# One kernel, two transformer blocks: loads of gates and activations in the expert down stage moved from SyncE's queue to ScalarE's

## The chip, the cores and the metric

The kernel runs on one core of one Trainium2 chip. The metric is the device time of one execution in microseconds (us); less is better. The time before is the median of three runs, 2463.1 us.

## What is computed

The reference is two transformer blocks on a sequence of 512 tokens with model width 1024, all in float32. The first block mixes tokens with attention and a gated linear scan and ends in a large sparse expert layer (`peer_ffn`); the second block has a pooling and gating mixer, a convolutional feed-forward layer and a gate. The change lies in the expert layer alone:

```
q = (xi @ w_q).reshape(n, 8, 2, 128)
s = einsum('nhpc,hpkc->nhpk', q, sub_keys)
...
idx  = ...                                   # 16 of 128*128 experts for each of 8 heads
gate = softmax(best_s)
act  = gelu(einsum('nd,nhkd->nhk', xi, u[idx]))
out  = einsum('nhk,nhkd->nd', gate * act, v[idx])
```

Each token uses 8 x 16 = 128 of the 16384 experts. `u` and `v` are tables of 16384 rows of 1024 numbers.

## The kernel before, in words

**Two ways through the expert layer.** The first 384 tokens (three tiles of 128) go a dense way: the activation of every expert is computed, and a matrix of gates, mostly zeros, is multiplied in. The experts are taken in 128 columns j of 128 experts. The last 128 tokens go a sparse way: `rows()` gathers for every token the rows of `u` and `v` it needs (`gather`, line 802, an indirect DMA issued by GpSimd) and VectorE multiplies and adds them (lines 815 and 823). These gathers run beside the dense work.

**Split operands.** A float32 matrix product is made of three products of float32r parts: high by high, high by low, low by high. Each weight tile of 512 KB is loaded raw by SyncE (`load_raw`, line 58, tile `wraw`), and `split` makes, in two halves each, the high part by a ScalarE cast (line 73, `whi`) and the low part by a VectorE subtraction (line 74, `wlo`). The raw tiles have 3 + 5 = 8 buffers in the expert layer, `whi` and `wlo` four half-tile buffers each, so two weight tiles are ready or in use at a time. `split` keeps its last cast in `c.step`, and `paced` makes an instruction wait for that cast.

**The up stage** (`route_and_up`) computes for j = 0 to 95 the activations gelu(x u_j) and stores them to a DRAM buffer `Ad`, four columns to a store (line 1022, from tile `ast`). The matrix of gates is built meanwhile and stored to a DRAM buffer `Gd`, 16 tokens to a store.

**The down stage** (`down`) walks through 160 steps in the order of `down_order`: eight "up" steps for a fresh block of columns, then 24 "down" steps for three kept blocks, then eight for the fresh one, four times over. An up step is 24 matmuls of 128 x 384 (line 97) and a Gelu on ScalarE (line 790, tile `fresh`). A down step is 18 matmuls of 128 x 512 (line 1105), which add w_j v_j into six PSUM banks, w_j being activations times gates. Each group of four down steps needs one `weigh`, emitted two steps ahead (`WEIGH = 2`): VectorE multiplies activations by gates (line 1070, tile `wt`), ScalarE casts the product (line 186, `wh`), VectorE makes its low part (line 187, `wl`). Before that, `load` brings the activations of the group back from `Ad` (line 1064, tile `at`, 768 KB, two buffers) and, once in two groups, the gates of a block of eight columns from `Gd` (line 1061, tile `gt`, 1536 KB in runs of 512 bytes, two buffers). `load` is emitted eight steps ahead (`LOAD = 8`), both loads go through SyncE's queue, and both are paced. Fresh blocks need no `at`: their activations are still in SBUF.

```
while to_load and to_load[0][0] - s <= LOAD:
    load(to_load.pop(0)[1])
while to_weigh and to_weigh[0][0] - s <= WEIGH:
    weigh(to_weigh.pop(0)[1])
```

**Order.** Each engine, and each engine's queue of DMA issues, works strictly in its own order. The order within an engine is fixed by the framework's scheduler when the kernel is built: it goes by the order of the code, but puts an instruction that it reckons ready before an earlier one that it does not. So SyncE issues the raw weight loads as soon as one of the eight buffers is reckoned free, ahead of their use, and the loads of `at` and `gt` stand between them in one queue.

Of the kernel before, what the change touches and what calls it, by code (L numbers as in the profile page):

```python
# [8 lines left out]
F32 = mybir.dt.float32  # L9
# [11 lines left out]
P = 128  # L21
# [163 lines left out]
def split_plain(c, hi, lo, x):  # L185
    c.nc.scalar.copy(hi, x)
    c.nc.vector.tensor_tensor(lo, x, hi.bitcast(F32), ALU.subtract)
# [545 lines left out]
DT = ND * P  # L733
GT = 16
NG = DT // GT
JG = 4
JG2 = 2 * JG
NS = 96
KEEP = 1
LOAD = 8  # L740
WEIGH = 2
ROWS = 4
AFTER = 4
# [13 lines left out]
def peer_block(c):  # L757
# [4 lines left out]
    with ExitStack() as ctx:  # L762
# [78 lines left out]
        with ExitStack() as vctx:  # L841
            down(c, vctx, aux, up, bank)
# [198 lines left out]
def down(c, ctx, aux, up, bank):  # L1041
    nc, tc, I, X = c.nc, c.tc, c.I, c.X
    wk = ctx.enter_context(tc.tile_pool(name="pv", bufs=2))
    acc = [aux(f"acc{i}") for i in range(2 * ND)]
    acts, gts, ws = {}, {}, {}
    rate = (2 * P - c.n_rows) / (NKEYS + (NKEYS - NS) - 8)
    due = 0.0

    def turn():
        nonlocal due  # L1050
        due += rate
        while due >= 1:
            next(c.rows, None)
            due -= 1

    def load(j):

        j0, b0 = j // JG2 * JG2, j % JG2
        if b0 == 0:
            gts[j0] = wk.tile([P, NG, JG2, GT], F32, name="gt")  # L1060
            c.paced(nc.sync.dma_start(out=gts[j0], in_=c.Gd[:, :, j0:j0 + JG2, :].rearrange("n i j g -> i n j g")))
        if j0 not in acts:
            ws[j] = wk.tile([P, JG, DT], F32, name="at")
            c.paced(nc.sync.dma_start(out=ws[j], in_=c.Ad[j // JG]))  # L1064

    def weigh(j):
        j0, b0 = j // JG2 * JG2, j % JG2
        at = acts[j0][:, b0:b0 + JG, :] if j0 in acts else ws[j]
        wt = wk.tile([P, JG, NG, GT], F32, name="wt", bufs=1)
        nc.vector.tensor_tensor(wt, at.rearrange("p j (n g) -> p j n g", g=GT),  # L1070
                                gts[j0][:, :, b0:b0 + JG, :].rearrange("p n j g -> p j n g"), ALU.mult)
        w = wt.rearrange("p j n g -> p j (n g)")
        ws[j] = [wk.tile([P, JG, DT], F32R, name=n) for n in ("wh", "wl")]
        split_plain(c, *ws[j], w)

    steps = [(what, j) for what, j0 in c.order for j in range(j0, j0 + JG2)]
    groups = [(s, j) for s, (what, j) in enumerate(steps) if what == "down" and j % JG == 0]
    to_load, to_weigh = list(groups), list(groups)
    n_done, batch = 0, []
    for s, (what, j) in enumerate(steps):  # L1080
        while to_load and to_load[0][0] - s <= LOAD:
            load(to_load.pop(0)[1])
        while to_weigh and to_weigh[0][0] - s <= WEIGH:
            weigh(to_weigh.pop(0)[1])
        if what == "up":
            if j % JG2 == 0:
                acts[j] = c.keep.tile([P, JG2, DT], F32, name="fresh")
            up(j, acts[j // JG2 * JG2][:, j % JG2, :])
            turn()
            continue  # L1090
        wh, wl = ws[j // JG * JG]
        vh, vl = next(c.peer_w)
        batch.append((j % JG, vh, vl))
        n_done += 1
        turn()
        if n_done == NKEYS - 1:
            continue

        last2 = n_done == NKEYS
        for hf in range(2):  # L1100
            for t in range(ND):
                tk = slice(t * P, (t + 1) * P)
                for bi, (jb, bh, bl) in enumerate(batch):
                    for pi, (x, y) in enumerate(((wh, bh), (wh, bl), (wl, bh))):
                        nc.tensor.matmul(acc[2 * t + hf], x[:, jb, tk], y.row(hf), start=n_done == 1 and pi == 0,  # L1105
                                         stop=last2 and bi == len(batch) - 1 and pi == 2)
        batch = []
    for _ in c.rows:
        pass
    for q in range(2):  # L1110
        for t in (ND, *range(ND)):
            if t < ND:
                y = wk.tile([P, 512], F32, tag=("at", "gt")[(q * ND + t) % 2], name="y")
                nc.scalar.copy(y, acc[2 * t + q])
            else:
                y = c.acc3[:, q * 512:(q + 1) * 512]
            o = bank("yt")
            for k in range(4):
                nc.tensor.transpose(o[:, k * P:(k + 1) * P], y[:, k * P:(k + 1) * P], c.ident)
            xs = X[:, 4 * q:4 * q + 4, t * P:(t + 1) * P]  # L1120
            nc.vector.tensor_tensor(xs, xs, o.rearrange("p (k n) -> p k n", k=4), ALU.add)
# [383 lines left out]
```

## Time and profile before

| | |
|---|---|
| runs | 2460.37, 2463.1, 2471.28 us; median 2463.1 |
| the profiled execution's own time | 2468.12 us |
| its span, from first to last instruction | 2466.4 us |
| TensorE busy (matmul) | 2402.0 us, 97% of the span |
| VectorE busy | 1758.2 us, 71% |
| ScalarE busy | 1194.7 us, 48% |
| GpSimd busy | 367.3 us, 15% |
| mean granted TensorE clock | 0.987 of full speed |

The profile counts an engine as busy while its instructions run; waiting, branching and issuing DMAs do not count. PE is TensorE's matmuls, PEld its weight loads, DVE VectorE, ACT ScalarE, POOL GpSimd, SP SyncE; a "q" behind an engine's name is its sequencer, which waits and issues DMAs. "a <- b" in a list of waits says that a stood idle until b was done. The down stage lies at about 962 to 1640 us of the span.

### The profile page before, as it was taken

The numbers are of one execution on the slowest core, as the hardware profiler recorded it, in microseconds if no ns is written. First come the engines' busy times: TensorE is split into PE (matmuls) and PEld (weight loads), VectorE is DVE, ScalarE is ACT, GpSimd is POOL, SyncE is SP. The second block draws the span as 40 slices with busy tenths as digits, with TensorE's granted clock in tenths as the row PEclk, the third lists the DMA queues.
The fourth block names the chain that finished last, engine by engine and source line by source line (L and its number), as shares of the span: only waits on it lengthen the run. The fifth ranks groups of instructions, "written<-read, shape, count | busy, mean of one in ns | idle before, by whom it ended". The sixth has DMA issues, their size and how long they took to land.

```text
span 2466.4 us, 34671 instructions
## 1 busy us (share of the span) xinstructions
PE 2402.0 (97%) x12603; PEld 2084.6 (85%) x12603; DVE 1758.2 (71%) x3426; ACT 1194.7 (48%) x2155; POOL 367.3 (15%) x260
## 2 busy tenths in 40 slices
PE   8999899999999999999999998999999999999998
PEld 7887578999999999888778788878888888888888
DVE  5775659999899886886676775866764456777436
ACT  5434553446788995433333333335433335544335
POOL 0000000001333323333242342420000000000000
PEclk9999999999999999999999999999999999999999
DMA  4210033356999999988888889953232232233332
GB/s 138 69 52 26 27 128 137 104 187 202 335 358 348 329 332 361 364 299 295 309 283 289 321 291 311 311 175 106 87 98 94 95 102 96 94 97 98 94 105 103
DMA packets 170297, 471.81 MB, mean 191 GB/s; under 512 B 14060, under 2 KB 66157, under 8 KB 166798
## 3 DMA queue, kind: packets, MB, share of 16 engines
q1 hardware_dynamic: 133262, 335.37, 39.8%
q0 software_dynamic: 36864, 134.23, 15.7%
q8 instruction: 99, 1.62, 0.3%
q14 instruction: 72, 0.59, 0.1%
HBM read 421.31 MB, written 48.23 MB: 190 GB/s over the span
## 4 chain that ended last, share of the span: by engine, by line
PE 62%; DMA 9%; issue 6%; DVE 5%; POOL 2%; ACT 1%; SPq 0%; DVEq 0%; POOLq 0%; ACTq 0%
PE mm L97 49%; PE acc L1105 8%; DMA at<-Ad 3%; DMA row<-in_v_t_dram,ev 3%; PE G L987 3%; POOL row L802 2%; DVE wlo L74 1%; DMA row<-in_peer_u_dram,eu 1%; DMA wraw<-in_v_t_dram 1%; DVE acc L823 1%; PE sc L886 1%; DMA gt<-Gd 1%; DVE row L815 0%; SPq L1064 0%; DVE eq L939 0%
## 5 line engine op out<-in xcount | busy, mean ns | idle before, releaser
L73 ACT CAST whi<-wraw 128x512 fp32r<-128x512 f32 (+3 forms) x902 | 547.4, 609 | 900.8 <-PE mm L97 521.3
L74 DVE TENSOR_TENSOR wlo<-wraw,whi 128x512 fp32r<-128x512 f32 (+3 forms) x902 | 595.4, 670 | 260.6 <-ACT whi L73 256.6
L97 PE MATMUL mm<-hi,whi 128*128 128x384 f32 (+3 forms) x2016 | 721.4, 363 | 16.3 <-ACT fresh L790 9.3
L97 PE MATMUL mm<-lo,whi 128*128 128x384 f32 (+3 forms) x2016 | 717.9, 361 | 0.7 <-DVE lo L182 0.5
L97 PE MATMUL mm<-hi,wlo 128*128 128x384 f32 (+3 forms) x2016 | 717.0, 361 | 0.4 <-DVE wlo L74 0.4
L97 PEld LDWEIGHTS mm<-hi,whi 128*128 128x128 f32 (+1 forms) x2016 | 376.3, 188 | 56.2 <-ACT fresh L790 10.2
L97 PEld LDWEIGHTS mm<-hi,wlo 128*128 128x128 f32 (+1 forms) x2016 | 376.0, 188 | 38.2 <-DVE wlo L74 1.7
L97 PEld LDWEIGHTS mm<-lo,whi 128*128 128x128 f32 (+1 forms) x2016 | 376.1, 188 | 38.1 <-issue 1.7
L1105 PE MATMUL acc<-wlo,wh 128*128 128x512 f32 x768 | 304.0, 396 | 20.9 <-DVE wlo L74 20.7
L802 POOL DMA_INDIRECT row<-in_peer_u_dram,eu x128 | 168.4, 1316 | 930.0 <-DMA wraw<-in_u_t_dram 544.4
L1105 PE MATMUL acc<-whi,wl 128*128 128x512 f32 x768 | 302.2, 394 | 0.0
L802 POOL DMA_INDIRECT row<-in_v_t_dram,ev x128 | 198.7, 1552 | 333.6 <-ACT whi L73 239.2
L1105 PE MATMUL acc<-whi,wh 128*128 128x512 f32 x768 | 248.1, 394 | 0.0
L823 DVE SCALAR_TENSOR_TENSOR acc<-row,act,acc 128x1024 f32<-128x1024 f32 x128 | 163.8, 1280 | 46.0 <-DMA row<-in_v_t_dram,ev 46.0
L1105 PEld LDWEIGHTS acc<-wlo,wh 128*128 128x128 f32 x768 | 146.3, 191 | 56.1 <-DVE wlo L74 25.7
L815 DVE SCALAR_TENSOR_TENSOR row<-row,hn 128x1024 f32<-128x1024 f32 x128 | 155.6, 1218 | 26.6 <-DMA row<-in_peer_u_dram,eu 26.3
L1105 PEld LDWEIGHTS acc<-whi,wh 128*128 128x128 f32 x768 | 146.0, 190 | 30.7
L1105 PEld LDWEIGHTS acc<-whi,wl 128*128 128x128 f32 x768 | 146.3, 190 | 30.3
L984 ACT ACTIVATE oa<-oa,tr 128x128 f32<-128x128 f32 x384 | 122.6, 393 | 21.5 <-DVE oa L982 21.1
L987 PE MATMUL G<-ob,oa 128*128 128x128 f32 x768 | 113.1, 277 | 1.2 <-ACT oa L984 1.2
L987 PEld LDWEIGHTS G<-ob,oa 128*128 128x128 f32 x768 | 108.9, 191 | 2.3 <-ACT oa L984 2.2
L988 ACT COPY gst<-G 128x512 f32<-128x512 f32 x96 | 102.1, 1070 | 16.1 <-PE G L987 15.2
(359 smaller groups left out, 3048.6 us busy)
## 6 DMA issues: line engine op xcount, KB each, us to landing
wraw<-in_u_t_dram SPq DMA_DIRECT2D x128, 512.0 KB, 5.3
wraw<-in_v_t_dram SPq DMA_DIRECT2D x128, 512.0 KB, 7.1
Gd<-gst SPq DMA_DIRECT2D x24, 1024.0 KB, 6.3
gt<-Gd SPq DMA_DIRECT2D x16, 1536.0 KB, 13.0
wraw<-in_w_up_dram SPq DMA_DIRECT2D x44, 512.0 KB, 3.4
Ad<-ast SPq DMA_DIRECT2D x24, 768.0 KB, 5.6
at<-Ad SPq DMA_DIRECT2D x24, 768.0 KB, 12.3
wraw<-in_w_pq_dram SPq DMA_DIRECT2D x16, 512.0 KB, 4.2
```

The lines of the kernel that those rows point to most:

```text
L73: self.step = nc.scalar.copy(hi[i], x)
L74: nc.vector.tensor_tensor(lo[i], x, hi[i].bitcast(F32), ALU.subtract)
L97: nc.tensor.matmul(o, a, b, start=first and ps == 0 and i == 0, stop=last and ps == 2 and i == n - 1)
L802: i = nc.gpsimd.indirect_dma_start(out=t, out_offset=None, in_=table, in_offset=bass.IndirectOffsetOnAxis(ap=idx[:, s:s + 1], axis=0))
L815: nc.vector.scalar_tensor_tensor(u, u, 1.0, hn, op0=ALU.mult, op1=ALU.mult, accum_out=c.act3[:, s:s + 1])
L823: nc.vector.scalar_tensor_tensor(c.acc3, v, c.act3[:, s:s + 1], c.acc3, op0=ALU.mult, op1=ALU.add)
L886: nc.tensor.matmul(o[:, t * P:(t + 1) * P], q[:, t * P:(t + 1) * P], keys[:, f, :], start=True, stop=True)
L984: nc.scalar.mul(oa[:, i, :], oa[:, i, :], tr[:, 2, b0 + i:b0 + i + 1])
L987: nc.tensor.matmul(o[:, i * P:(i + 1) * P], oa[:, i, :], ob[:, i, :], start=True, stop=True)
L988: nc.scalar.copy(st[:, :, b0 - t0:b0 - t0 + TB].rearrange("p j n -> p n j"), o.rearrange("p (n j) -> p n j", n=TB))
L1105: nc.tensor.matmul(acc[2 * t + hf], x[:, jb, tk], y.row(hf), start=n_done == 1 and pi == 0, stop=last2 and bi == len(batch) - 1 and pi == 2)
```

## The change

The function `load` and its distance `LOAD` go. In its place are `load_gates` and `load_acts`, each of which takes the next load from a list. Both issue their DMA from ScalarE's queue and neither is paced. Two blocks of gates and two groups of activations are loaded ahead of the first step; after that, each `weigh` of a kept group is followed by the load of activations for the kept group after next (into the buffer that it has just read), and each second `weigh` of a block by the load of gates for the block after next. The name of the change also says that the weights' low parts stay in halves; the code before has them in halves, and no line of the diff touches them.

```diff
-LOAD = 8
...
-    def load(j):
-
-        j0, b0 = j // JG2 * JG2, j % JG2
-        if b0 == 0:
-            gts[j0] = wk.tile([P, NG, JG2, GT], F32, name="gt")
-            c.paced(nc.sync.dma_start(out=gts[j0], in_=c.Gd[:, :, j0:j0 + JG2, :].rearrange("n i j g -> i n j g")))
-        if j0 not in acts:
-            ws[j] = wk.tile([P, JG, DT], F32, name="at")
-            c.paced(nc.sync.dma_start(out=ws[j], in_=c.Ad[j // JG]))
+    def load_gates():
+        j0 = gts_due.pop(0)
+        gts[j0] = wk.tile([P, NG, JG2, GT], F32, name="gt")
+        nc.scalar.dma_start(out=gts[j0], in_=c.Gd[:, :, j0:j0 + JG2, :].rearrange("n i j g -> i n j g"))
+
+    def load_acts():
+        j = ats_due.pop(0)
+        ws[j] = wk.tile([P, JG, DT], F32, name="at")
+        nc.scalar.dma_start(out=ws[j], in_=c.Ad[j // JG])
 
     def weigh(j):
...
         split_plain(c, *ws[j], w)
 
+        if j < NS and ats_due:
+            load_acts()
+        if b0 and gts_due:
+            load_gates()
+
     steps = [(what, j) for what, j0 in c.order for j in range(j0, j0 + JG2)]
     groups = [(s, j) for s, (what, j) in enumerate(steps) if what == "down" and j % JG == 0]
-    to_load, to_weigh = list(groups), list(groups)
+    to_weigh = list(groups)
+    ats_due, gts_due = [j for _, j in groups if j < NS], [j for _, j in groups if j % JG2 == 0]
+    for f in (load_gates, load_acts, load_acts, load_gates):
+        f()
     n_done, batch = 0, []
     for s, (what, j) in enumerate(steps):
-        while to_load and to_load[0][0] - s <= LOAD:
-            load(to_load.pop(0)[1])
         while to_weigh and to_weigh[0][0] - s <= WEIGH:
             weigh(to_weigh.pop(0)[1])
```

## Rows read from the trace of the kernel before

**Rows 1.** The page's first part: busy time and share of the span by engine.
```profile
PE 2402.0 (97%) x12603; PEld 2084.6 (85%) x12603; DVE 1758.2 (71%) x3426; ACT 1194.7 (48%) x2155; POOL 367.3 (15%) x260
```

**Rows 2.** Stretch, length, busy us (count) of PE PEld DVE ACT POOL, clock, DMA share, GB/s.
```profile
962.00:1640.00 678.00, 647.87 (x2971) 554.38 (x2970) 491.74 (x564) 247.37 (x374) 239.17 (x156) 0.98 0.89 307
996.00:1119.00 123.00, 123.00 (x544) 101.86 (x543) 96.48 (x121) 46.41 (x68) 42.34 (x32) 1.00 0.93 324
```

**Rows 3.** Who waited for whom in the down stage: us, times, longest us.
```profile
ACT whi L73 <- PE acc L1105: 296.1, 197, 8.4
DVE wt L1070 <- DMA at<-Ad: 68.0, 13, 10.0
...
DVE acc L823 <- DMA row<-in_v_t_dram,ev: 46.0, 33, 6.5
...
ACT wh L186 <- DVE wt L1070: 28.3, 8, 7.5
...
PE acc L1105 <- DVE wlo L74: 20.7, 9, 5.2
...
DVE wt L1070 <- DMA gt<-Gd: 11.4, 3, 4.0
...
PE mm L97 <- ACT fresh L790: 9.3, 3, 4.1
```

**Rows 4.** Six short stretches without matmuls; columns as in rows 2.
```profile
1138.80:1142.90 4.10, 0.00 (x0) 0.00 (x0) 4.10 (x4) 2.42 (x4) 0.16 (x1) 1.00 0.63 251
1178.30:1183.50 5.20, 0.02 (x1) 0.00 (x0) 2.36 (x3) 0.23 (x1) 0.00 (x0) 0.78 0.69 275
1323.90:1325.90 2.00, 0.02 (x1) 0.00 (x0) 2.00 (x3) 2.00 (x4) 0.15 (x1) 1.00 0.90 356
1359.60:1364.60 5.00, 0.00 (x0) 0.00 (x1) 2.41 (x3) 0.39 (x1) 0.00 (x0) 0.76 1.00 400
1498.90:1502.00 3.10, 0.03 (x1) 0.00 (x0) 3.10 (x4) 2.36 (x4) 0.10 (x1) 1.00 0.65 260
1537.20:1541.00 3.80, 0.02 (x1) 0.00 (x0) 2.33 (x3) 0.45 (x1) 0.00 (x0) 0.82 0.92 367
```

**Rows 5.** First and last of five slow-clock stretches behind them, and one at full clock.
```profile
1143.60:1147.00 3.40, 3.40 (x13) 3.40 (x12) 3.40 (x6) 1.30 (x3) 2.56 (x2) 0.52 0.43 64
...
1541.20:1546.40 5.20, 5.20 (x13) 4.04 (x14) 5.20 (x7) 0.62 (x1) 3.05 (x1) 0.50 0.58 202
1547.00:1552.20 5.20, 5.20 (x25) 4.27 (x24) 4.35 (x6) 2.93 (x4) 1.81 (x1) 1.00 0.61 235
```

**Rows 6.** SyncE's queue in order of time: start us, us, what it issued.
```profile
963.34 0.33 SPq L1022 DMA_DIRECT2D Ad<-ast  x1
...
968.87 0.38 SPq L1061 DMA_DIRECT2D gt<-Gd  x1
969.30 7.18 SPq L1064 DMA_DIRECT2D at<-Ad  x1
...
1091.65 31.18 SPq L58 DMA_DIRECT2D wraw<-in_u_t_dram  x8
...
1123.36 7.53 SPq L1064 DMA_DIRECT2D at<-Ad  x1
```

**Rows 7.** Line 1064, loads of activations: ns min/median/max of the issue, then landing.
```profile
L1064 SPq DMA_DIRECT2D at<-Ad x24: 327/2174/9269, 969.3 to 1578.6; - x24
...
DMA to landing us min/median/max: 4.9/12.3/18.4
```

**Rows 8.** Line 1061, loads of gates: the same two rows.
```profile
L1061 SPq DMA_DIRECT2D gt<-Gd x16: 377/380/387, 968.9 to 1594.0; - x16
...
DMA to landing us min/median/max: 10.0/13.0/16.4
```

**Rows 9.** ScalarE in order of time: the last Gelu of the up stage.
```profile
962.83 0.49 ACT L790 ACTIVATE ast<-mm 128x384 f32<-128x384 f32 x1
```

**Rows 10.** The gathered rows of the sparse way, from 1142 to 1640 us.
```profile
DMA to landing us min/median/max: 4.1/7.5/11.8
```

## The prediction

> **What bounds the kernel now.** I first read the page's busy times: TensorE works for 97% of the span [rows 1], so only time in which it stands still or runs slowly can be won. Then the busy times by stretch: in the down stage TensorE is busy for 647.87 of 678 us, so some 30 us are idle; yet from 996 to 1119 us the same work runs without a gap [rows 2]. The list of waits says what ends the idle time: 20.7 us end with a VectorE low part of a weight (9 times) and 9.3 us with a ScalarE Gelu (3 times) [rows 3]. Neither of these is slow in itself. Above them in the list VectorE stands 68.0 us, 13 times, before its product `wt` for the activations `at` to land, and 11.4 us for the gates [rows 3]. VectorE works in order, so the low parts of the weights stand behind `wt`; ScalarE's cast `wh` waits for `wt` too (28.3 us, at most 7.5), and with it the Gelus behind it. The reader should see two hops: a late load holds VectorE, and TensorE starves a few us later.
>
> Why the load is late shows in SyncE's queue: around 1100 us it spends 31.18 us on eight raw weight loads, which wait for free buffers, and only then, at 1123.36, comes to `at`, whose issue itself takes 7.53 us because it stands behind the gates' load [rows 6]. That issue takes 327 ns when nothing is in the way and up to 9269 behind `gt`; landing takes 12.3 us at the median and 18.4 at most [rows 7].
>
> **What the change takes away.** Six gaps of TensorE follow such a late `at`: 4.10 + 5.18 + 1.98 + 5.00 + 3.07 + 3.78 = 23.1 us [rows 4]. After five of them the granted clock is at 0.50 (1.2 instead of 2.4 GHz) for a stretch; these add up to 20.4 us. At that clock 13 matmuls are recorded in 5.2 us against 25 at full clock [rows 5], so half of the 20.4 is lost, 10.2 us. Together 33.3 us. In the new order the activations for a group are issued after the product two groups earlier, about eight down steps ahead; 544 recorded matmuls in 123 us, 18 to a step [rows 2], are 4.1 us a step, so 33 us ahead, against a landing of 12.3 (at most 18.4). The gates come three groups ahead, 49 us, against 13.0 (at most 16.4) [rows 7, 8]. Across the eight up steps of a fresh block the lead is larger still. Nor does either load stand behind SyncE's waits. So I take the whole 33 us away. The lower bound is nothing, if landing and not issue was what came late (first rival).
>
> **What it adds on ScalarE in the steady state.** Forty issues move from SyncE to ScalarE: 16 of the gates at 0.38 us [rows 8] and 24 of the activations at 0.33, as long as they don't follow a `gt` closely [rows 7]; in the new order `at` goes ahead of `gt` and the next `at` comes 16 us later, beyond the longest hold of 9.3. That is 6 + 8 = 14 us of ScalarE, which stands 296.1 us in this stage only waiting for TensorE before its casts [rows 3]. I cost it at nothing; without that cover it would be at most 14. The wait that each load brings (its buffer free after `wt`) is one that the cast `wh` has anyway, so what is queued behind it (casts and Gelus) is held no longer, if VectorE is on time. SyncE loses 40 issues and their holds; its raw weight loads come sooner, and eight buffers covered them before: nothing.
>
> **What it adds at the start.** Four loads, gates, activations, activations, gates, 4.5 MB, stand in a row in ScalarE's queue. The first can't go before the last store of the up stage has left its buffer: SyncE issued that store at 963.34 and the first gates' load at 968.87; the activations behind it took 7.18 us to issue [rows 6]. How long ScalarE is held depends on where the scheduler puts the four among the casts, which no row shows. If they go where their wait is over, the hold is about 7.2 us; if they follow the last Gelu of the up stage (962.83 + 0.49 [rows 9]), it lasts from 963.3 to about 977, 13.7 us. A ScalarE wait of at most 7.5 us before `wh` gave a TensorE wait of at most 4.1 [rows 3], so about 3.4 us are covered: the gap is 3.8 to 10.3 us, plus 1.7 to 2.6 for the slow clock after it. Were the four spread out, it would be 0. I take 6, nearest to the row with the 7.5 us wait, whose length the likelier placing has, and keep 0 to 13 for the range.
>
> **What is late next.** VectorE also waits for gathered rows, 46.0 us in 33 waits [rows 3]. Without the waits for `at` it comes to its rows sooner, so a part moves there. The stretch from 996 to 1119 shows what is left: no gap at 324 GB/s [rows 2], and the shortened stage needs 678 x 307 / 645 = 323 GB/s (an estimate from the same rows). I set 3 us for it, between 0 and the 27 of the first rival.
>
> **The sum.** 33 - 6 - 3 = 24 us. The profiled execution took 2468.1 us (span 2466.4), 5.0 above the median of the runs; 2468.1 - 24 = 2444.1, and beside the median 2439.
>
> A measurement of this kernel can tell about 0.5%, 12.3 us, from no change: the band is 2450.8 to 2475.4.
>
> Weighed against a rule: the landing times [rows 7] and the hold in the queue [rows 6] are two causes that the list of waits doesn't separate. The Trainium skill (DMA: Bandwidth & Descriptors, "Issuing engines are not separate DMA queues") says that DMAs from all issuing engines run on the same 16 engines and interleave, so that issuing from several saves only the sequencer's time to initiate them. By that the sum would be near 0 and the time near 2463, if the sequencer's time were only the 0.33 us of an issue; here it includes the 31 us behind other loads' waits, which is why I stay with the trace's sum.
>
> **The rivals.**
>
> *Contention takes the wait over.* The loads are hidden, but the gathers are not. For it: the stage runs at 307 GB/s with a DMA share of 0.89 [rows 2], and three queues then share the engines where two did. While a gates' load is under way (16 x 13.0 = 208 us [rows 8]) a gather could take half as long again, 11.3 us instead of 7.5; 11.8 has been seen [rows 10]. If the 33 rows that already wait come 1.9 us later each, that is 63 us of VectorE; the 79.4 us it stood for `at` and `gt` cost TensorE 33, 0.42 per us, so 27 are lost, and 33 - 6 - 27 = 0: 2463. Against it: the gapless stretch at 324 GB/s.
>
> *ScalarE is held behind every load of gates (slower).* On SyncE the activations behind a gates' load were held: the first of twelve for 7.18 us [rows 6], 6.4 on average over the twelve. If casts and Gelus behind it on ScalarE are held as a DMA is, 16 holds of 6.4, less 3.4 covered, plus 1.7 for the slow clock, cost 75 us: 2463 + 75 - 33 = 2505. It decides as soon as a hold exceeds 3.4 + 33 / 16 - 1.7 = 3.8 us. Against it: a gates' load itself occupies the queue for 0.38 us [rows 8], and only a DMA was seen held.
>
> *More falls away.* The four loads spread themselves out and the row waits shrink with the bursts: the remaining 6.9 us of idle go too; 2463 - 33 - 7 = 2423.
>
> *The change doesn't do what it says*: low parts are in halves before and after; that part costs and brings nothing, so it has no time of its own.
>
> **How the numbers follow.** The forecast has 0.61, with more falling away 0.07, contention 0.20, the hold 0.12. Of contention I count 0.02 as partial and still faster. Faster by over 0.5%: 0.70; within: 0.18; slower: 0.12. Forecast 2439; its own range is 2424 (no cost at the start, nothing late next) to 2450 (13 at the start, 7 more on rows). The range wanted reaches from 2424 to 2468, which takes in contention with 5 us more at the start and leaves out the hold and little below.
>
> **What would show it.** Right: VectorE's waits for `at` and `gt` gone from the list, from 79 us to under 10; one gap of TensorE near 970 us with ScalarE held by the four issues; gaps after 1119 us under 10 us in all; row waits near 46 us. Wrong: row waits above 100 us (contention); ScalarE idle behind each gates' issue and regular gaps of TensorE every 32 us (the hold); or `at` still late although issued early.

## The result, and the profile after

The changed kernel takes 2430.44 us (median of five runs, 2427.75 to 2435.47) against 2463.1 before; the ratio is 0.9866 with a 95% interval of 0.9842 to 0.989. The forecast was 2439 with a range of 2424 to 2468. The span of the profiled execution falls from 2466.4 to 2433.5 us.

The busy times by stretch of the changed kernel (columns as in rows 2): first the down stage but for its last microsecond (it now begins 3 us earlier), then six short stretches of it.

```profile
959.00:1630.00 671.00, 661.14 (x3072) 568.63 (x3071) 502.38 (x575) 256.33 (x389) 213.48 (x156) 0.99 0.89 311
993.10:996.40 3.30, 0.00 (x0) 0.00 (x0) 0.00 (x0) 0.64 (x2) 0.00 (x0) 1.00 1.23 301
998.00:1001.20 3.20, 3.20 (x9) 2.46 (x9) 2.86 (x4) 2.39 (x4) 0.00 (x0) 0.50 0.71 208
1457.40:1461.10 3.70, 0.02 (x1) 0.00 (x0) 1.87 (x3) 1.82 (x2) 1.61 (x1) 1.00 1.04 403
1462.00:1465.40 3.40, 3.40 (x12) 3.40 (x11) 3.40 (x5) 0.62 (x1) 0.00 (x0) 0.50 1.19 305
1558.60:1561.10 2.50, 0.00 (x0) 0.00 (x0) 1.89 (x2) 0.00 (x0) 0.94 (x1) 0.97 0.89 352
1561.20:1564.30 3.10, 3.10 (x8) 2.42 (x8) 3.07 (x4) 0.19 (x1) 0.00 (x0) 0.50 0.58 204
```

None of the six gaps of [rows 4] is left. Three new ones stand there, 3.3, 3.7 and 2.5 us, each with 3.1 to 3.4 us at half clock behind it. The list of waits of the changed kernel in the down stage says what ends them:

```profile
DVE acc L822 <- DMA row<-in_v_t_dram,ev: 43.2, 25, 5.6
...
PE mm L97 <- DVE wlo L74: 3.8, 1, 3.8
...
PE acc L1110 <- ACT whi L73: 3.3, 1, 3.3
...
PE acc L1110 <- DVE wlo L74: 2.6, 1, 2.6
...
PE mm L97 <- ACT fresh L789: 0.2, 1, 0.2
```

Lines 790, 802, 823, 1070 and 1105 of the kernel before are 789, 801, 822, 1069 and 1110 here; 1061 (gates) and 1064 (activations) are 1058 and 1063. VectorE's waits of 68.0 and 11.4 us for `at` and `gt` [rows 3] are gone altogether; its wait for gathered rows stands at 43.2 us, where it was 46.0.

The loads now stand in ScalarE's queue. Its order of time at the start of the stage:

```profile
967.84 0.39 ACTq L1058 DMA_DIRECT2D gt<-Gd  x1
968.06 0.49 ACT L789 ACTIVATE fresh<-mm 128x384 f32<-128x384 f32 x1
968.28 5.71 ACTq L1063 DMA_DIRECT2D at<-Ad  x2
974.03 0.44 ACTq L1058 DMA_DIRECT2D gt<-Gd  x1
974.59 1.14 ACT L73 CAST whi<-wraw 128x512 fp32r<-128x512 f32 x2 [6.05 <-PE mm L97]
...
985.66 10.01 ACTq L1063 DMA_DIRECT2D at<-Ad  x1
995.76 1.14 ACT L73 CAST whi<-wraw 128x512 fp32r<-128x512 f32 x2 [8.68 <-DMA wraw<-in_v_t_dram]
```

ScalarE is held twice. The first hold, between 968.6 and 974.6, costs TensorE 0.2 us. The second is 10.01 us long, behind the second gates' load, and ends in the gap at 993.1. (The profile puts the idle time before the cast down to a raw load; what stood in front of the cast in ScalarE's queue is the issue above it, which ended at 995.67, 0.09 us before the cast.)

Loads of activations and of gates, issue in ns and landing in us, answering to [rows 7, 8]:

```profile
L1063 ACTq DMA_DIRECT2D at<-Ad x24: 326/327/10006, 968.3 to 1520.4; - x24
...
DMA to landing us min/median/max: 4.3/7.0/15.8
```
```profile
L1058 ACTq DMA_DIRECT2D gt<-Gd x16: 377/448/701, 967.8 to 1520.7; - x16
...
DMA to landing us min/median/max: 18.0/22.4/27.9
```

The activations land sooner, 7.0 instead of 12.3 us. Before, half of them stood directly behind a gates' load, and where the trace tells their landing, those took 12.3 to 18.4 us and the others 4.9 to 13.1. The gates take longer, 22.4 instead of 13.0 us; with the same code on SyncE's queue (e1_sync_queue below) it is 15.0. Why they land later is not shown. With three groups of lead nobody waits for that.

### The profile page after: what moved, and what is told of

Its sections match the earlier page's. It is cut to its first block, busy times and chain, and to the rows that moved or that the text cites. A ratio compares the mean times of both kernels' runs of the same rounds, so it can differ in the third digit from the quotient of the medians.

```text
span 2433.5 us, 34668 instructions
## 1 busy us (share of the span) xinstructions
PE 2389.3 (98%) x12603; PEld 2078.8 (85%) x12603; DVE 1760.7 (72%) x3426; ACT 1194.8 (49%) x2155; POOL 342.3 (14%) x260
## 5 line engine op out<-in xcount | busy, mean ns | idle before, releaser
L801 POOL DMA_INDIRECT row<-in_peer_u_dram,eu x128 | 160.4, 1253 | 933.8 <-DMA wraw<-in_u_t_dram 541.9
L1110 PE MATMUL acc<-whi,wh 128*128 128x512 f32 x768 | 231.0, 391 | 3.3 <-ACT whi L73 3.3
L801 POOL DMA_INDIRECT row<-in_v_t_dram,ev x128 | 181.7, 1419 | 322.2 <-ACT whi L73 192.3
L822 DVE SCALAR_TENSOR_TENSOR acc<-row,act,acc 128x1024 f32<-128x1024 f32 x128 | 163.7, 1279 | 43.7 <-DMA row<-in_v_t_dram,ev 43.2
## 6 DMA issues: line engine op xcount, KB each, us to landing
gt<-Gd ACTq DMA_DIRECT2D x16, 1536.0 KB, 22.4
```

Source lines behind the costliest of these rows:

```text
L801: i = nc.gpsimd.indirect_dma_start(out=t, out_offset=None, in_=table, in_offset=bass.IndirectOffsetOnAxis(ap=idx[:, s:s + 1], axis=0))
L822: nc.vector.scalar_tensor_tensor(c.acc3, v, c.act3[:, s:s + 1], c.acc3, op0=ALU.mult, op1=ALU.add)
```

## The experiments

**Queue or lead.** The change does three things at once: it changes the queue, takes the pacing away and gives the loads a place right behind the product that frees their buffer. Four kernels separate them.

*e1_sync_queue*: the changed kernel, both loads back on SyncE's queue.

```diff
-        nc.scalar.dma_start(out=gts[j0], ...
+        nc.sync.dma_start(out=gts[j0], ...
-        nc.scalar.dma_start(out=ws[j], ...
+        nc.sync.dma_start(out=ws[j], ...
```

> The new code and its lead of two groups, with both loads back on SyncE's queue. Theory A (the gain comes from leaving SyncE's queue, where a load stands behind waits of the weight loads): loads late again, VectorE waits for at and gt 40 us or more, time 2445 to 2463. Theory B (the gain comes from the longer lead): VectorE waits for at and gt under 10 us and time 2425 to 2440, as the changed kernel.

Measured: 2423.43 us (2422.23 to 2427.7), ratio 0.9848 (0.9818 to 0.9877). The whole gain is there without ScalarE's queue. The stage has no gap:

```profile
962.00:1618.00 656.00, 655.91 (x3072) 565.04 (x3071) 501.84 (x573) 256.88 (x390) 208.28 (x156) 1.00 0.90 318
```

*e2_old_lead_scalar*: the kernel before, both loads from ScalarE's queue.

```diff
-            c.paced(nc.sync.dma_start(out=gts[j0], ...
+            c.paced(nc.scalar.dma_start(out=gts[j0], ...
-            c.paced(nc.sync.dma_start(out=ws[j], ...
+            c.paced(nc.scalar.dma_start(out=ws[j], ...
```

> The kernel before with both loads issued from ScalarE's queue, old lead of eight steps, paced as before. Theory A (queue): the load no longer stands behind weight loads, waits for at under 15 us, time 2430 to 2445. Theory B (lead): waits for at stay near 60 us and time 2455 to 2470, or above, because at directly follows gt on ScalarE and holds its casts: up to twelve holds of 6.4 us less 3.4 covered, 36 us.

Measured: 2472.73 us (2459.88 to 2483.72), ratio 1.0037 (1.0014 to 1.006). The queue alone gains nothing, and it makes the loads no earlier: the fifth load of gates goes at 1138.41 us here, at 1122.92 before, though no weight load stands in ScalarE's queue. VectorE's waits for `at` do fall (to 19.6 us) and those for `gt` rise to 19.5. All twelve activations' loads that follow gates are now held on ScalarE, for 5.7 to 9.9 us each; the waits of this run put nine of ScalarE's waits down to it ("issue"):

```profile
ACT whi L73 <- issue: 67.1, 9, 10.4
...
DVE wt L1070 <- DMA at<-Ad: 19.6, 6, 4.8
DVE wt L1070 <- DMA gt<-Gd: 19.5, 4, 7.2
...
PE acc L1105 <- ACT whi L73: 13.3, 7, 4.0
```

*e7_unpaced*: the kernel before without the two calls of `c.paced`, nothing else.

```diff
-            c.paced(nc.sync.dma_start(out=gts[j0], ...))
+            (nc.sync.dma_start(out=gts[j0], ...))
-            c.paced(nc.sync.dma_start(out=ws[j], ...))
+            (nc.sync.dma_start(out=ws[j], ...))
```

> The kernel before with the pacing of both loads taken away, queue and lead kept. If the pacing (a wait for the last weight cast) made the loads late, the waits for at fall below 20 us and the time to 2430 to 2440. Theory A: the loads stand behind the same weight loads, waits for at 50 us or more, time within 8 us of 2463. Theory B: the loads may move up to where their buffer is free, which is two groups ahead as in the changed kernel, so 2430 to 2445.

Measured: 2428.01 us (2422.57 to 2429.35), ratio 0.9862 (0.9834 to 0.989), 2 us under both ranges that expected a gain; VectorE waits for neither load. Theory A falls. Two calls taken away do what the change does. The place to compare is the first kept block after the second set of up steps, with the fifth load of gates and the seventh of activations. Before, they go right after the eight raw loads of [rows 6], the activations at 1123.36 and the gates just ahead of them:

```profile
1122.92 0.39 SPq L1061 DMA_DIRECT2D gt<-Gd  x1
```

SyncE's queue in this run (the first line is the seventh load of activations, the third the fifth of gates):

```profile
1034.49 0.33 SPq L1064 DMA_DIRECT2D at<-Ad  x1
1036.29 12.58 SPq L58 DMA_DIRECT2D wraw<-in_v_t_dram  x4
1052.01 0.38 SPq L1061 DMA_DIRECT2D gt<-Gd  x1
1052.44 3.50 SPq L1064 DMA_DIRECT2D at<-Ad  x1
1056.03 25.48 SPq L58 DMA_DIRECT2D wraw<-in_v_t_dram  x8
1084.60 0.38 SPq L1061 DMA_DIRECT2D gt<-Gd  x1
```

Here the gates go 71 us and the activations 89 us earlier, ahead of those eight raw loads and of others, and as early as in the changed kernel (1055.15 and 1037.52). The loads share the queue with the same waits for weight buffers, and that does no harm once their places in it are early enough. This run alone doesn't tell the pacing from the lead, since without the pacing the loads also move up; the next one does.

*e8_sync_paced*: e1_sync_queue with the pacing put back on both loads.

```diff
-        nc.sync.dma_start(out=gts[j0], ...)
+        c.paced(nc.sync.dma_start(out=gts[j0], ...))
-        nc.sync.dma_start(out=ws[j], ...)
+        c.paced(nc.sync.dma_start(out=ws[j], ...))
```

> The new code on SyncE's queue, as in the run e1_sync_queue (2423.4 us), with the pacing put back on both loads. Theory C (what made the loads late was the pacing together with its place eight steps ahead: it kept the scheduler from moving a load up to where its buffer is free): here the pacing names a cast only two steps before the buffer is free, so the loads stay early, waits for at and gt under 15 us, 2420 to 2432. Theory D (any pacing makes the loads late): waits of 40 us or more, 2445 to 2465.

Measured: 2430.07 us (2423.84 to 2432.34), ratio 0.9857 (0.9823 to 0.9891); VectorE waits 3.5 us for `at` and none for `gt`, and the fifth load of gates goes at 1064.65. So pacing as such isn't the fault (theory D falls): pacing a load at a point eight steps ahead of its use is. In the kernel before, that point came after the eight raw loads had been placed in the queue, and the wait for the cast kept the scheduler from placing the load before them, though its buffer was free by then: in e7_unpaced the same gates' load was issued at 1052.01. The loads are early if either the pacing goes (e7_unpaced) or the place in the code is earlier (this run), and late only with both.

**What ScalarE's queue costs.** *e3_gates_first*: the changed kernel with the two loads behind a second product in the other order.

```diff
-        if j < NS and ats_due:
-            load_acts()
         if b0 and gts_due:
             load_gates()
+        if j < NS and ats_due:
+            load_acts()
```

> The changed kernel with the gates' load put ahead of the activations' load after each second product, so that at stands directly behind gt on ScalarE's queue in every kept block. If a DMA behind gt holds ScalarE's casts: eleven or twelve holds of 5 to 10 us, each a gap of 2 to 5 us of TensorE and 1.7 us of slow clock, time 2465 to 2505. If the casts pass a held DMA: no holds, 2425 to 2436.

Measured: 2463.33 us, ratio 0.9996 (0.9978 to 1.0014), 1.7 us under the range that the hold would give: the whole gain is lost again. Beside the two holds at the start, eleven activations' loads behind gates are held, for 3.9 to 9.3 us. The waits of this run, and one of its holds on ScalarE:

```profile
ACT whi L73 <- issue: 69.1, 9, 10.4
...
PE acc L1110 <- ACT whi L73: 22.5, 8, 5.0
```
```profile
1195.48 0.38 ACTq L1058 DMA_DIRECT2D gt<-Gd  x1
1195.89 9.26 ACTq L1063 DMA_DIRECT2D at<-Ad  x1
1205.24 1.66 ACT L73 CAST whi<-wraw 128x512 fp32r<-128x512 f32 x3 [10.44 <-issue]
```

Casts do wait behind a held DMA, and the order of two lines decides over 33 us (2463.3 against 2430.4). On SyncE the same succession is harmless: e7_unpaced has an `at` directly behind a `gt` four times, held for 3.5 to 6.5 us, and no gap.

*e4_start_sync*: the changed kernel with only the first four loads on SyncE's queue.

```diff
-    def load_gates():
+    def load_gates(q=nc.scalar):
...
-        nc.scalar.dma_start(out=gts[j0], ...
+        q.dma_start(out=gts[j0], ...
...
     for f in (load_gates, load_acts, load_acts, load_gates):
-        f()
+        f(nc.sync)
```

> The changed kernel with only the first four loads on SyncE's queue, all later ones on ScalarE's. If the two holds of ScalarE at the start (6 and 10 us in the changed kernel) are what the queue costs, the gap of 3.3 us near 996 us goes and the time falls by about 5 us, to 2421 to 2428; the two gaps after late gathers (3.8 and 2.6 us) stay. If the start costs nothing, 2428 to 2435.

Measured: 2428.87 us (2425.51 to 2433.95), ratio 0.986 (0.9827 to 0.9894): above the first expected range, inside the one for a start that costs nothing, and not to be told from the changed kernel. But the start still costs something: the hold moved instead of going: the activations at 1006.97, behind the first gates that ScalarE issued itself, took 9.30 us to issue, and TensorE had gaps of 1.6 us (to 999.1) and 2.3 us (to 1017.3). The two gaps after late gathers, expected to stay, were not there; one of 0.9 us stood at 1432.

*e5_gates_sync* and *e6_acts_sync*: only one of the two loads on ScalarE's queue.

```diff
-        nc.scalar.dma_start(out=gts[j0], ...
+        nc.sync.dma_start(out=gts[j0], ...
```
```diff
-        nc.scalar.dma_start(out=ws[j], ...
+        nc.sync.dma_start(out=ws[j], ...
```

> The changed kernel with the gates on SyncE's queue and the activations on ScalarE's. No load follows gates on ScalarE, so no holds; the gates stand in line with the weight loads, so they land in about 15 us instead of 22 and the gathers have a queue less beside them. Theory E (the gates' own queue slows the gathers): longest landing of a gather back to 12 us, no gaps of TensorE in the stage, 2418 to 2427. Otherwise the two gaps after late gathers stay and it is 2425 to 2432.

> The changed kernel with the activations on SyncE's queue and the gates alone on ScalarE's. No holds on ScalarE but for gates behind gates at the start. Theory E: the gates still land in 20 us or more, gathers land late up to 15 us, one to three gaps of 2 to 4 us, 2424 to 2432. If the holds were the whole cost of ScalarE's queue: no gaps, 2418 to 2425.

Measured: 2430.68 us (2424.73 to 2433.55), ratio 0.9855 (0.9823 to 0.9887), and 2433.22 us (2430.28 to 2433.78), ratio 0.9871 (0.9841 to 0.9901), the second above both of its ranges. Theory E falls as it was put: with the gates in line on SyncE one late gather still made a gap of 3.7 us, and with the gates on ScalarE (landing in 22.8 us from 996 to 1600 us) the longest gather took 11.5 us and made none. With both loads on SyncE, e8_sync_paced has gaps of 2.2 and 2.6 us after late gathers. In e6_acts_sync the one gap is at the start: the second gates' load, directly behind the first, held ScalarE for 10.85 us and TensorE for 4.8.

**Again, side by side.** The changed kernel, e1_sync_queue and e7_unpaced, unchanged, on one chip with five rounds.

> The changed kernel again, beside the two below on one chip. If the two gaps after late gathers (near 1461 and 1561 us) belong to the order of its instructions, they stand in this trace again; if they come and go, they do not. ScalarE's holds at the start (6 and 10 us) and the gap near 996 us must be there again. Time 2427 to 2433.

> The new code with SyncE's queue again. If ScalarE's queue costs the changed kernel its start holds, this one is 4 to 8 us below it, 2420 to 2426; if the difference of the first runs was chance, within 3 us of it.

> The kernel before without the pacing of its two loads, again: two calls taken away and nothing else. If this is the whole gain, it stands beside the run on SyncE's queue within 3 us and 4 to 8 us below the changed kernel; its first runs spread from 2422.6 to 2429.4.

Measured: 2437.33 us (ratio 0.9892, 0.9865 to 0.9919), 2423.91 us (0.9842, 0.9817 to 0.9867) and 2424.89 us (0.9842, 0.9819 to 0.9864). The first is 4 us above its range, so the others are some 13 us below it, not the 4 to 8 expected. The intervals of the first and the others touch, but the order is the same as in the first runs. Over all runs the medians are 2433.4 (11 runs of the changed kernel), 2423.9 (10) and 2425.3 (9). In the changed kernel's trace the start holds are back (4.97 and 10.21 us) with a gap of 4.8 us at 1002; of the late gathers one made a gap near 1468 and none near 1561. r2_sync_again has no gap in the stage, r3_unpaced_again one of 2.2 us near 1457. So the late gathers come and go, most often near 1460 us.

The traces show one mark of them. In the changed kernel:

```profile
1446.50 4.37 POOL L801 DMA_INDIRECT row<-in_v_t_dram,ev  x1 [0.30 <-issue]
...
1459.23 1.28 DVE L822 SCALAR_TENSOR_TENSOR acc<-row,act,acc 128x1024 f32<-128x1024 f32 x1 [5.57 <-DMA row<-in_v_t_dram,ev]
```

GpSimd was busy 4.37 us with this gather, where the median is 1.26 (spans on GpSimd are rough), and the row landed 12.6 us after the start, when VectorE had stood for 5.57. The gaps near 1460 in e5_gates_sync, r1_changed_again and r3_unpaced_again follow gathers of 4.37, 4.37 and 4.23 us in the same way, and the changed kernel's gap at 1558.6 one of 7.16. e1_sync_queue, e6_acts_sync, e7_unpaced and r2_sync_again have no gather of over 3 us after 1230 us, and no such gap. It isn't the only way: the two gaps of e8_sync_paced follow gathers of 1.1 to 1.3 us. Nor is it enough: the kernel before has twelve gathers of over 3 us there. What makes them long stays open.

## Why the prediction was right, and where its reason was not

**The amount taken away was right.** The six gaps and five slow stretches, 33.3 us, are all gone, and VectorE's 79 us with them.

**The reason given for it was half wrong.** The step "Nor does either load stand behind SyncE's waits" put the late issue down to SyncE's queue. The runs put another thing in its place: the load's pacing at eight steps ahead. The queue alone brought 2472.7 us, the earlier place in the code alone 2430.1 (e8_sync_paced), the pacing taken away alone 2428.0, and these two together, on SyncE's queue, 2423.4. The observation in [rows 6], eight raw loads ahead of the gates, was right; that the order is made by the scheduler and can be changed without leaving the queue was overlooked. The rule weighed in the prediction, that issuing from several engines saves only the sequencer's time (the Trainium skill, DMA: Bandwidth & Descriptors, "Issuing engines are not separate DMA queues"), agrees with the time of e2_old_lead_scalar (ratio 1.0037) for the queue, though there the holds on ScalarE are in that time too. What it leaves out is that the other half of the change was no matter of queues.

**The start: right in size, wrong in place.** 6 us were taken for it. Measured are 0.2 + 3.3 us of gaps and 1.6 us for 3.2 us at half clock, 5.1 in all. But the four first loads themselves, a hold of 6 us, cost almost nothing; what cost was the next load of activations, 11.6 us behind the second gates. The step that said that the next `at` comes "beyond the longest hold of 9.3" failed there: the hold ended 21.6 us after the gates' issue, and these gates landed after 25.3 us. (That the slower landing made the hold longer is likely, not shown.) In the steady state the step held by a narrow margin: 13 to 19 us behind the gates the issue took 0.33 us, twice 1.3 to 1.4 us, and once 3.9 in r1_changed_again.

**What is late next: about right.** 3 us were taken. The other gaps, 6.9 us and 1.7 of slow clock before, became 3.7 + 2.5 us and two slow stretches of 3.4 us, 9.6 in all; that is 1 us more.

**The sum** of these is 33.3 - 5.1 - 1.0 = 27.2 us, against a difference of the spans of 32.9. 3.0 of the rest lie ahead of the down stage, which no line of the change touches: the last Gelu of the up stage comes at 959.79 instead of 962.83 [rows 9]; in the other runs it comes between 959.8 and 970.7, so these 3 us are luck. The last 2.7 us lie in the down stage: from that Gelu to its last matmul it takes 701.2 us before and 671.3 after. They are less than two executions of one kernel differ by, and their cause stays open. (The stage before ends at 1664 us, not at about 1640; no gap lies in what is left out, so the sum is untouched.) The forecast of 24 us came out 8.7 short of the medians' 32.7; the larger parts of that are this rest and the 2.9 us by which the start and the rows cost less than taken. Without gaps the stage takes 656.1 us (e1_sync_queue), so the changed kernel still leaves 15 us in it.

The range has a slip: no cost at the start and nothing late next is 2463 - 33 = 2430, not the 2424 that stands as its lower end; 2424 needs the remaining 6.9 us of idle time too. That 2430 is also what was measured is luck: costs of 6.1 us were there, and 5.7 us came from elsewhere.

**The rivals.** Contention fell: without gaps e1_sync_queue moves 318 GB/s through the stage, VectorE's row waits are 32.4 us, less than before, and in the changed kernel itself they are 43.2 at 311 GB/s. The hold was real as a mechanism and was priced at 75 us for 16 of them; e3_gates_first has eleven in the steady state and loses 33 us against the changed kernel, 3.0 us each where 4.7 were set. The changed kernel escapes it by the order of two lines. "More falls away", 2423, is what e1_sync_queue reaches.

The two best versions are e1_sync_queue and e7_unpaced, which can't be told apart: 2424 to 2425 us, 38 to 39 us below the kernel before and some 8 to 10 below the changed one. The second is the kernel before with two calls less.

## What to carry to other kernels

When a load is late, look first at where its issue stands in its queue and what put it there: here a wait given to it on purpose, to slow it down, at a point too close to its use. An extra wait doesn't only delay an instruction, it also tells a scheduler not to place it earlier. A computing engine's queue is no free place for a transfer of many small pieces: here a DMA that followed it on ScalarE's queue at once or up to 13 us later was held for 4 to 11 us, and the engine's work behind that DMA too. From 13 us on most went through in 0.33 us, so if such a transfer must be there, leave it time before the next DMA.

## What the runs showed of the hardware that was not expected

- A load of 1536 KB in runs of 512 bytes takes 0.38 to 0.70 us to issue in the changed kernel and lets other instructions pass, but holds the next DMA of the same queue. The hold is no fixed time: behind the first gates it ended 7.6 us after their issue on SyncE (before) and some 6 us on ScalarE (changed kernel); behind the second gates on ScalarE, which landed after 25.3 us, 21.6 us.
- The same code has the gates land in 15.0 us at the median on SyncE's queue (e1_sync_queue) and in 22.4 on ScalarE's. But the queue alone doesn't make it: in e3_gates_first, on ScalarE's queue too, the median is 13.3. There gates with a held load directly behind them landed in 9.5 to 14.9 us (nine that the trace tells), and three without in 17.2 to 24.4. Why stays open.
- ScalarE standing for 6.05 us cost TensorE 0.2 us, and for 8.68 us 3.3, so 5.9 and 5.4 us were covered there, more than the 3.4 worked out from the waits before `wh`. In r1_changed_again 8.9 us cost 4.8.
